# Output projection and first gate of a two-layer decoder trunk: plain products in place of block products

## The chip, the cores and the metric

One core of one Trainium2 chip runs the whole program in one launch. Times are device microseconds (us), the median over runs. TensorE is PE, VectorE is DVE, ScalarE is ACT, GpSimd is POOL, and SP issues most of the DMAs.

## The reference

Two layers over 1024 positions of width 1024, float32 throughout. `u` is a root-mean-square norm of `h`:

```
proj  = u @ w_in[i]                        # 8 forgetting-attention heads, 8 retention heads
mixed = concat(fox_attention(...), silu(rg) * group_norm(retention(...)))
h = h + mixed @ w_out[i]                   # output projection, 1024 x 1024
up = rms_norm(h, ffn_norm_w[i]) @ w_up[i]  # 1024 x 5632, halves a and g
h = h + (gelu(causal_conv3(a)) * g) @ w_down[i]
gate = sigmoid(rms_norm(h, ple_norm_w[i]) @ w_ple_gate[i])   # 1024 x 1024
h = h + gate * (p[i] @ w_ple_proj[i])
```

After the second layer there is a last norm of `h`.

## The kernel before

Everything lies feature-major: `h` is eight slices of 128 features x 1024 positions. A float32 product is made of three products of rounded parts, high by high, low by high and high by low, so every operand is split into two (`xh`, `xl`; `wh`, `wl`; `uh`, `ul`; `dh`, `dl`): the high part by a cast on ACT, the low part by a subtraction, on DVE or POOL as the table behind `E(name, i)` says (one letter per index: V is DVE, G is POOL).

There are two kinds of product. A **plain product** (`dense_fm`) makes one output slice of 128 features out of 8 input slices: 8 x 6 matmuls of 512 columns into a PSUM tile `d` of 128x1024; its weights come ready in order from `weights()`, which loads and splits them four ahead. A **block product** (`g_parts`, `parts`) makes two output slices (a "quarter" q of four) with seven half-size products in place of eight. The seven, `NAMES`, each take for every pair of input slices three matmuls of 512 columns. The weight side is made by a `Line` of steps (`Fixed`): raw weights `wr`, sums `ws` on POOL, then high part `wh` on ACT and low part `wl` on DVE. The moving side of a pair of slices is a `Joined`: four builds with subtractions (`t`) and splits (`x`, `xh`, `xl`) on ACT and DVE. `join` adds the seven half results, 128x512 each, out of PSUM into `h` on DVE; `form` puts them together in a new tile.

A layer runs: input projections (plain) woven with attention and retention by `weave`, where the tuple `DENSE` is the order of the dense pieces and `SPANS` says between which positions in it each of the four attention and four retention pairs is spread; the output projection; the MLP's up product (block); its down product in four groups of input pairs (block); the gate; and the norm's sums of squares (`Stats`, tiles `hsq` and `ssq`) along the way. The second layer's gate is plain, with moving sides by `make_u` (`uh`, `ul` of a slice); the first layer's is a block product. The output projection is done in two halves of its input: the attention heads' half, `g_out`, is the last piece "wo0" of `DENSE` and so woven with the last retention pair; the retention heads' half follows after it. `h` goes to DRAM (`hs_dram`) and is read back for the down product, and once more for the first gate. The tile framework's scheduler decides the order on each engine out of the order in which the program is written and the room that tiles need.

Nearly all instructions are issued by one helper at line 145, so groups in the profile are told apart by their tiles.

Of the kernel before, what the change touches and what calls it, by code (L numbers as in the profile page):

```python
# [9 lines left out]
F32 = mybir.dt.float32  # L10
# [7 lines left out]
DEPTH = 2  # L18
# [16 lines left out]

DENSE = ("fi1", "rv0", "fi2", "fv1", "fi3", "ri0", "rv1", "rg0", "ri1", "ri2", "rg1", "ri3", "ep0", "em0", "wo0")
SPANS = ((6, 42.6), (42.6, 79.9), (85.9, 123.5), (130.4, 145.5), (138.9, 199.2), (194.7, 197.7), (217.3, 254.5), (251.1, 300.0))

# [121 lines left out]
def trunk(ctx, tc, ap):  # L160
# [48 lines left out]
    def weight_order():  # L209
        V, G_ = nc.vector, nc.gpsimd  # L210
        for l in range(DEPTH):
            qk = lambda j: (ap["wqk"][l, j], KC, P, E("qk", j))
            tm = lambda j: [(ap["wtm"][l, j, i], 4, 256, E("tm", 2 * j + i)) for i in range(2)]
            fv0 = [(ap["wfv"][l][:, a:b, :], b - a, FVW, G_) for a, b in FVK]
            specs = {"ep": lambda i: [], "wo": lambda i: [],
                     "fi": lambda i: [qk(i), qk(4 + i)], "fv": lambda i: tm(0), "ri": lambda i: [qk(8 + i), qk(12 + i)],
                     "rv": lambda i: tm(1 + i), "rg": lambda i: tm(3 + i),
                     "em": lambda i: [(ap["wproj"][l, j], 8, P, E("em", j)) for j in range(2)]}
# [693 lines left out]
    for l in range(DEPTH):  # L912
# [119 lines left out]

        def hand(now, then):

            def after(n):
                for m in now:
                    m.drop(n)
                for m in then:
                    m.build(n)
            return after  # L1040

        def specs():
            for half in range(2):
                for q in range(4):
                    yield ap["wout"][l, half, q], 2
# [6 lines left out]
            if l + 1 < DEPTH:  # L1052
                for q in range(4):
                    yield ap["wgate"][l, q], 4

        def g_out():

            nonlocal line, u, rb
            u = rb = None
            del pr[:], ret_tab[:]  # L1060
            line = Line(specs())
            for p in range(2):
                mx.append(Joined(mixed[2 * p], mixed[2 * p + 1]))
                mixed[2 * p:2 * p + 2] = [None, None]
            for q in range(4):
                for m in (2 * q, 2 * q + 1):
                    h[m] = G("h")
                    nc.sync.dma_start(h[m], h_dram[m])
                to = h[2 * q:2 * q + 2]
                yield from g_parts(line, mx, lambda name, s: join(name, s, to))  # L1070

        fox_ops, ret_ops, ret_v, ret_tab, vst, tail = {}, {}, {}, [], [], []
        pr, mx, h, line = [], [], [None] * KC, None
        pp = dr.tile([KC, P, T], F32, name="pp")
        raw = []
        for name in ("qs", "ks"):
# [3 lines left out]
            if name == "qs":  # L1080
# [8 lines left out]
                  "ep": lambda i: g_load_embed(),  # L1089
                  "em": lambda i: g_embed(), "wo": lambda i: g_out()}  # L1090
        units = [(a, e, 27.0, lambda i=i: fox(i)) for i, (a, e) in enumerate(SPANS[:4])]
# [4 lines left out]
        ret_v.clear()  # L1096
        del vst[:]


        def scales(which, p):  # L1100
            return nw[:, which, 2 * p:2 * p + 1], nw[:, which, 2 * p + 1:2 * p + 2], minus[:, which, 2 * p + 1:2 * p + 2]

        stats = Stats()
        mx = [Joined(mixed[2 * p], mixed[2 * p + 1]) for p in (2, 3)]
        mixed = None
        u = []
        hs_dram = dr.tile([KC, P, T], F32, name="hs")
        for q in range(4):
            to = h[2 * q:2 * q + 2]
            parts(line, mx, lambda name, s: join(name, s, to), hand(mx, []) if q == 3 else None)  # L1110
            u.append(Joined(*to, scales(2 * NW_FFN + l, q)))
            for m in (2 * q, 2 * q + 1):
# [3 lines left out]
        to = None  # L1116

# [50 lines left out]
        for g, mx in enumerate(stored):  # L1168
            then = stored[g + 1] if g + 1 < len(stored) else []
            for q in range(4):  # L1170
                if g == 0:
                    for m in (2 * q, 2 * q + 1):
                        h[m] = G("h")
                        nc.sync.dma_start(h[m], hs_dram[m])
                to = h[2 * q:2 * q + 2]
                if q == 3:
                    for m in then:
                        m.load(0)

                def after(n):  # L1180
                    for m in mx:
                        m.drop(n)
                    for m in then:
                        m.build(n)
                        if n < 3:
                            m.load(n + 1)
                    if not then and not ends:
                        u[2].build(n)
# [10 lines left out]
                if not then and not ends:  # L1199

                    for m in range(2 * q - 2 if q == 3 else 2 * q, 2 * q + 2):
                        if q != 2:
                            h[m] = None
        mx = then = stored = to = None


        if not ends:
            nstats = Stats()
            h_dram = dr.tile([KC, P, T], F32, name="hd")
            rb = None  # L1210
            old, u = u, []
            for q in range(4):
                sg = [G("sg") for i in range(2)]
                for m in (2 * q, 2 * q + 1):
                    h[m] = G("h")
                    nc.sync.dma_start(h[m], hs_dram[m])

                def scale_s(i):
                    nonlocal rb, stats
                    if rb is None:  # L1220
                        _, rb = stats.finish()
                        stats = None
                    return rb

                def after(n):
                    for m in old:
                        m.drop(n)
                    if n:
                        u.extend(make_u(h[m], nw[:, 2 * NW_ATTN + l + 1, m:m + 1]) for m in (2 * n - 2, 2 * n - 1))
                    if n == 2:  # L1230
                        fetch()
                parts(line, old, lambda name, s: form(name, s, sg, scale_s), after if q == 3 else None)
                for i in range(2):
                    m = 2 * q + i
                    pt = G("ppt")
                    nc.sync.dma_start(pt, pp[m])
                    nc.scalar.activation(sg[i], sg[i], AF.Sigmoid)
                    nc.gpsimd.tensor_tensor(sg[i], sg[i], pt, op=ALU.mult)
                    nc.vector.tensor_tensor(h[m], h[m], sg[i], op=ALU.add)
                    if q == 3:  # L1240
                        u.append(make_u(h[m], nw[:, 2 * NW_ATTN + l + 1, m:m + 1]))
                    nstats.add(h[m], sg[i])
                    nc.sync.dma_start(h_dram[m], h[m])
                    if q == 3:
                        h[m] = None
                sg = pt = None
            stats, nstats = nstats, None
            h = rb = old = None

    fetch()  # L1250

# [126 lines left out]
```

## Time and profile before

| | |
|---|---|
| median of 3 runs | 2899.47 us (2892.65 to 2899.89) |
| the profiled execution | 2898.59 us, of which the span is 2896.8 us |
| mean granted TensorE clock | 0.97 of full speed |
| PE busy | 2717.5 us, 94%, 13718 matmuls |
| DVE busy | 2086.6 us, 72% |
| ACT, POOL busy | 1226.5 us (42%), 902.0 us (31%) |

The shares are means over stages that differ. The stages lie about so in the span: layer 0's attention and retention up to 580 us, the second half of its output projection 580 to 690, its MLP to 1290, its gate to 1460; layer 1's to 2028, 2028 to 2137, to 2737, and its gate and the last norm behind that.

### The profile page before, as it was taken

The page shows a single profiled execution, that of the slowest core. Times are in us where ns is not written, and L with a number is a line of the kernel's source. Part 1 is how long each engine was busy: PE and PEld are TensorE (multiplying, and loading weights), DVE is VectorE, ACT ScalarE, POOL GpSimd, SP SyncE. Part 2 cuts the span into 40 slices and gives each one's busy share as a digit, 9 for nine tenths or more (in the row PEclk, how much of TensorE's full clock was granted, in tenths as well). Part 3 has the DMA queues.
Part 4 walks back from the last instruction along what each step waited for, and adds up shares of the span by engine and source line. Part 5 has one row for each costly group of instructions (what it writes and reads, how often), then busy time and mean ns, then how long its engine had stood idle before and what let it go on. Part 6 is the DMA issues. An engine that isn't in the chain of part 4 may idle for free. (4 is left out here: it accounts for less than half of the span.)

```text
span 2896.8 us, 36327 instructions
## 1 busy us (share of the span) xinstructions
PE 2717.5 (94%) x13718; PEld 2263.5 (78%) x13718; DVE 2086.6 (72%) x3031; ACT 1226.5 (42%) x1824; POOL 902.0 (31%) x652
## 2 busy tenths in 40 slices
PE   8988999978999998997889989999799999989998
PEld 7887989757888887775678879897578888867776
DVE  4565645898887778779745556458978877787786
ACT  4354543444344333435434545424443433434352
POOL 3222332223233323434432222322232333234240
PEclk9999999999999999998989999999999999999999
DMA  5333122422323236433533331224223232364242
GB/s 161 88 81 95 54 61 71 158 76 95 109 99 113 95 132 213 153 95 120 178 91 88 81 97 52 62 72 154 77 95 109 99 112 96 137 208 151 87 146 98
DMA packets 116864, 315.77 MB, mean 109 GB/s; under 512 B 13520, under 2 KB 34512, under 8 KB 116688
## 3 DMA queue, kind: packets, MB, share of 16 engines
q1 hardware_dynamic: 113616, 305.05, 32.4%
q10 hardware_dynamic: 3072, 8.39, 1.2%
q8 instruction: 108, 1.77, 0.3%
q14 instruction: 68, 0.56, 0.1%
HBM read 210.04 MB, written 69.80 MB: 97 GB/s over the span
## 5 line engine op out<-in xcount | busy, mean ns | idle before, releaser
L145 POOL TENSOR_TENSOR ws<-wr 128x512 f32<-128x512 f32 (+2 forms) x192 | 285.7, 1495 | 1049.6 <-PE d L145 520.6
L145 PE MATMUL s<-xh,wh 128*128 128x512 f32 x936 | 377.8, 406 | 25.6 <-ACT wh L145 13.2
L145 PE MATMUL d<-xh,wh 128*128 128x512 f32 x936 | 374.8, 404 | 20.2 <-DVE h L145 12.6
L145 PE MATMUL s<-xl,wh 128*128 128x512 f32 x936 | 377.4, 403 | 11.2 <-DVE xl L145 11.2
L145 PE MATMUL s<-xh,wl 128*128 128x512 f32 x936 | 372.0, 403 | 6.1 <-DVE wl L145 5.7
L145 PE MATMUL d<-xl,wh 128*128 128x512 f32 x936 | 373.6, 399 | 2.4 <-DVE xl L145 2.4
L145 PE MATMUL d<-xh,wl 128*128 128x512 f32 x936 | 370.6, 399 | 0.0
L145 POOL TENSOR_TENSOR ws<-ws,wr 128x512 f32<-128x512 f32 (+2 forms) x192 | 262.9, 1370 | 104.2 <-issue 55.6
L145 PE MATMUL d<-x,w 128*128 128x512 f32 x936 | 246.2, 399 | 22.4 <-ACT x L145 8.8
L145 ACT CAST wh<-ws 128x1024 fp32r<-128x1024 f32 (+2 forms) x192 | 168.5, 888 | 219.8 <-POOL ws L145 203.6
L145 DVE TENSOR_TENSOR wl<-ws,wh 128x1024 fp32r<-128x1024 f32 (+2 forms) x192 | 218.3, 1146 | 40.7 <-ACT wh L145 31.9
L145 PE MATMUL d<-dh,uh 128*128 128x256 f32 (+1 forms) x768 | 222.1, 290 | 22.8 <-DVE vst L145 11.2
L145 PEld LDWEIGHTS s<-xh,wh 128*128 128x128 f32 x936 | 180.0, 192 | 76.3 <-ACT wh L145 20.5
L145 PEld LDWEIGHTS d<-xh,wh 128*128 128x128 f32 x936 | 178.9, 191 | 71.5 <-DVE h L145 21.0
L145 PEld LDWEIGHTS d<-x,w 128*128 128x128 f32 x936 | 175.3, 190 | 71.1 <-ACT x L145 10.1
L145 PEld LDWEIGHTS s<-xl,wh 128*128 128x128 f32 x936 | 180.5, 193 | 54.8 <-DVE xl L145 14.3
L145 PEld LDWEIGHTS s<-xh,wl 128*128 128x128 f32 x936 | 180.0, 192 | 54.5 <-DVE wl L145 13.3
L145 PE MATMUL d<-dl,uh 128*128 128x256 f32 (+1 forms) x768 | 221.8, 289 | 0.0
L145 PE MATMUL d<-dh,ul 128*128 128x256 f32 (+1 forms) x768 | 220.8, 288 | 0.0
L145 PE MATMUL d<-uh,dh 128*128 128x512 f32 (+1 forms) x584 | 197.6, 407 | 18.1 <-ACT dh L145 11.1
L145 PEld LDWEIGHTS d<-xl,wh 128*128 128x128 f32 x936 | 179.6, 192 | 43.7 <-DVE xl L145 3.0
L145 PEld LDWEIGHTS d<-xh,wl 128*128 128x128 f32 x936 | 178.9, 191 | 42.2
(209 smaller groups left out, 5863.3 us busy)
## 6 DMA issues: line engine op xcount, KB each, us to landing
wr<-in_wup_dram SPq DMA_DIRECT2D x88, 512.0 KB, 3.8
zz<-zd SPq DMA_DIRECT2D x66, 512.0 KB, 3.7
wr<-in_wdown_dram SPq DMA_DIRECT2D x48, 384.0 KB, 4.2
zd<-z SPq DMA_DIRECT2D x66, 256.0 KB, 2.0
dr<-in_wqk_dram SPq DMA_DIRECT2D x32, 512.0 KB, 3.5
hs<-h SPq DMA_DIRECT2D x24, 512.0 KB, 2.6
h<-hs SPq DMA_DIRECT2D x24, 512.0 KB, 4.8
zd<-t SPq DMA_DIRECT2D x22, 512.0 KB, 3.9
```

The source lines that it names most:

```text
L145: ins = f(*[bare(v) for v in a], **{n: bare(v) for n, v in k.items()})
```

## The change

The output projection of both layers and the gate of the first become plain products. "wo0" leaves `DENSE` and the last retention pair's span in `SPANS` shrinks with it. All eight `mixed` slices are split into `mxh`, `mxl` (four low parts on POOL, by an entry that the table has, `mx="GVVGVGGV"`), and eight plain products follow; after each odd slice the block sides (`Joined`) for the MLP are built for the two finished slices, and the MLP's weight `Line` begins at slice 4. Behind the down product both layers now make the gate's sides with `make_u`, keep `h` in place, and call `fetch()` at the third quarter. In the gate, the result of the first two slices is copied out of PSUM by ACT, and the product with `ppt` is on DVE. The weights are laid out to match.

```
-DENSE = (..., "ri3", "ep0", "em0", "wo0")
-SPANS = (..., (217.3, 254.5), (251.1, 300.0))
+DENSE = (..., "ri3", "ep0", "em0")
+SPANS = (..., (217.3, 254.5), (251.1, 259.3))
...
+            yield from [(ap["wout"][l, m], KC, P, E("wo", m)) for m in range(KC)]
             yield None
-            for i in range(len(PIECES) if l + 1 == DEPTH else 0):
-                yield from [(ap["wlast"][0, m], KC, P, E("gate%d" % l, i * KC + m)) for m in range(KC)]
+            for i in range(len(PIECES) if l + 1 == DEPTH else 1):
+                yield from [(ap["wgate"][l, m], KC, P, E("gate%d" % l, i * KC + m)) for m in range(KC)]
...
+        mx = []
+        for c in range(8):
+            mx.append((G("mxh", F32R), G("mxl", F32R)))
+            split(*mx[c], mixed[c], E("mx", c))
+            mixed[c] = None
+        mixed = None
         stats = Stats()
-        mx = [Joined(mixed[2 * p], mixed[2 * p + 1]) for p in (2, 3)]
...
-        for q in range(4):
-            to = h[2 * q:2 * q + 2]
-            parts(line, mx, lambda name, s: join(name, s, to), hand(mx, []) if q == 3 else None)
-            u.append(Joined(*to, scales(2 * NW_FFN + l, q)))
-            for m in (2 * q, 2 * q + 1):
-                stats.add(h[m], G("hsq"))
-                nc.sync.dma_start(hs_dram[m], h[m])
-                h[m] = None
+        for m in range(KC):
+            h[m] = G("h")
+            nc.sync.dma_start(h[m], h_dram[m])
+            if m == 4:
+                line = Line(specs())
+            elif m > 4:
+                line.step()
+            d = dense_fm(weights(), mx)
+            if m == KC - 1:
+                mx = None
+            nc.vector.tensor_tensor(h[m], d, h[m], op=ALU.add)
+            nc.sync.dma_start(hs_dram[m], h[m])
+            stats.add(h[m], G("hsq"))
+            if m % 2:
+                s1 = slice(m - 1, m)
+                s2 = slice(m, m + 1)
+                u.append(Joined(h[m - 1], h[m], (nw[:, 2 * NW_FFN + l, s1], nw[:, 2 * NW_FFN + l, s2], minus[:, 2 * NW_FFN + l, s2])))
+                h[m - 1:m + 1] = [None, None]
...
                 if not then:
-                    if ends:
-                        u += [make_u(h[m], nw[:, 2 * NW_PLE + l, m:m + 1]) for m in (2 * q, 2 * q + 1)]
-                    else:
-                        u.append(Joined(*to, scales(2 * NW_PLE + l, q), q != 2))
+                    u += [make_u(h[m], nw[:, 2 * NW_PLE + l, m:m + 1]) for m in (2 * q, 2 * q + 1)]
                     for m in (2 * q, 2 * q + 1):
                         stats.add(h[m], G("hsq"), None, E("hsq", m))
-                        if not ends:
-                            nc.sync.dma_start(hs_dram[m], h[m])
...
+                    if q == 2:
+                        fetch()
...
-                parts(line, old, lambda name, s: form(name, s, sg, scale_s), after if q == 3 else None)
-                for i in range(2):
-                    m = 2 * q + i
-                    pt = G("ppt")
-                    nc.sync.dma_start(pt, pp[m])
-                    nc.scalar.activation(sg[i], sg[i], AF.Sigmoid)
-                    nc.gpsimd.tensor_tensor(sg[i], sg[i], pt, op=ALU.mult)
-                    nc.vector.tensor_tensor(h[m], h[m], sg[i], op=ALU.add)
...
+            for m in range(KC):
+                pt = G("ppt")
+                nc.sync.dma_start(pt, pp[m])
+                d = dense_fm(weights(), u)
+                if m == 0:
+                    _, rb = stats.finish()
+                    stats = None
+                sg = G("sg")
+                if m < 2:
+                    nc.scalar.copy(sg, d)
+                nc.vector.tensor_tensor(sg, sg if m < 2 else d, rb, op=ALU.mult)
+                nc.scalar.activation(sg, sg, AF.Sigmoid)
+                nc.vector.tensor_tensor(sg, sg, pt, op=ALU.mult)
+                nc.vector.tensor_tensor(h[m], h[m], sg, op=ALU.add)
+                then.append(make_u(h[m], nw[:, 2 * NW_ATTN + l + 1, m:m + 1]))
+                nstats.add(h[m], sg)
+                nc.sync.dma_start(h_dram[m], h[m])
+                h[m] = None
```

What it moves on the engines, at three places. The first is PE in layer 0, in the last retention pair (`qn`, `kz`, `rv`, `state`, `sm` are its chunks). Before:

```order
L145 MATMUL d<-xh,wh 128x512
L145 MATMUL d<-xl,wh 128x512
L145 MATMUL d<-xh,wl 128x512
L145 MATMUL s<-qn,kz_5178 128x128
L145 MATMUL s<-qn,kz_5179 128x128
L145 MATMUL s<-rv,kt 128x128
L145 MATMUL s<-state,qn 128x128
L145 MATMUL s<-rv,sm 128x64 x2
L145 MATMUL d<-xh,wh 128x512
L145 MATMUL d<-xl,wh 128x512
L145 MATMUL d<-xh,wl 128x512
L145 MATMUL d<-xh,wh 128x512
```

and with the change, some of the same chunks:

```order
L145 MATMUL s<-qn,kz_5179 128x128
L145 MATMUL s<-state,qn 128x128
L145 MATMUL s<-rv,kt 128x128
L145 MATMUL s<-rv,sm 128x64 x2
L145 MATMUL s<-state,qn 128x128
L145 MATMUL s<-rv,sm 128x64 x2
L145 MATMUL s<-qn,kz_5178 128x128
L145 MATMUL s<-qn,kz_5179 128x128
L145 MATMUL s<-rv,kt 128x128
L145 MATMUL s<-state,qn 128x128
L145 MATMUL s<-rv,sm 128x64 x2
L145 MATMUL s<-qn,kz_5178 128x128
```

The 512-column products of the output projection (`xh`, `wh`) that stood between the chunks are gone, and chunk follows chunk.

The second is DVE in layer 0 in the second half of the output projection (the number behind a tile's name is its buffer). Before, half results (128x512) going into several slices of `h` with the block side of the first slices between them:

```order
L145 TENSOR_TENSOR h_5533<-h_5533,d_6003 128x512
L145 TENSOR_TENSOR h_5396<-h_5396,s_5903 128x512
L145 TENSOR_TENSOR h_5394<-h_5394,d_5892 128x512
L145 SCALAR_TENSOR_TENSOR x_5965<-h_5394,nw_84,x_5965 128x512
L145 TENSOR_TENSOR h_5535<-h_5535,s_6014 128x512
L145 TENSOR_TENSOR h_5533<-h_5533,d_6003 128x512
L145 TENSOR_TENSOR h_5394<-h_5394,s_5903 128x512
L145 TENSOR_TENSOR h_5396<-h_5396,d_5892 128x512
L145 SCALAR_TENSOR_TENSOR t2_5970<-h_5394,nw_84,t34_5971 128x512
```

and with the change, one plain result (128x1024) for a slice, the low part of a weight, and then the block side of the pair:

```order
L145 TENSOR_TENSOR h_5689<-d_5697,h_5689 128x1024
L145 TENSOR_TENSOR dl_5851<-dr_5848,dh_5850 128x1024
L145 SCALAR_TENSOR_TENSOR t2_5756<-h_5689,minus_66,t2_5756 128x512
L145 SCALAR_TENSOR_TENSOR t34_5757<-h_5689,nw_84,t34_5757 128x512
L145 TENSOR_TENSOR ssq_5537<-ssq_5537,hsq_5748 128x1024
L145 SCALAR_TENSOR_TENSOR xl_5764<-h_5689,nw_84,xh_5763 128x512
L145 SCALAR_TENSOR_TENSOR t34_5757<-h_5689,minus_66,t2_5756 128x512
L145 SCALAR_TENSOR_TENSOR xl_5771<-h_5689,nw_84,xh_5770 128x512
L145 TENSOR_TENSOR xl_5755<-t2_5756,xh_5754 128x1024
L145 TENSOR_TENSOR xl_5764<-t34_5757,xh_5763 128x512
```

One sum of 128x1024 has taken the place of the half sums, and a whole side follows in one piece.

The third is PE at the end of the first gate with the change, where the next layer's first products begin (`uh_11465` and `ul_11466` are made from the gate's last slice; rows of the same product for other slices stand ahead of these):

```order
L145 MATMUL d_11480<-uh_11396,dh_11407 128x512 x2
L145 MATMUL d_11480<-ul_11397,dh_11407 128x512 x2
L145 MATMUL d_11480<-uh_11396,dl_11408 128x512 x2
L145 MATMUL d_11562<-uh_10981,dh_11476 128x512 x2
L145 MATMUL d_11562<-ul_10982,dh_11476 128x512 x2
L145 MATMUL d_11562<-uh_10981,dl_11477 128x512 x2
L145 MATMUL d_11480<-uh_11465,dh_11407 128x512 x2
L145 MATMUL d_11562<-uh_11051,dh_11476 128x512 x2
```

The next layer's second product `d_11562` begins before the first, `d_11480`, has its last input. In the change's order 48 matmuls of 512 columns stand between the gate's last matmul and the first use of `uh_11465`.

## Rows read from the trace of the kernel before

**Rows 1.** The page's first line and its busy times with shares of the span and instruction counts.

```profile
span 2896.8 us, 36327 instructions
...
PE 2717.5 (94%) x13718; PEld 2263.5 (78%) x13718; DVE 2086.6 (72%) x3031; ACT 1226.5 (42%) x1824; POOL 902.0 (31%) x652
```

**Rows 2.** Busy time of each engine by stretch: from:to in us, length, then PE (with the count of matmuls), PEld, DVE, ACT and POOL busy us with counts, mean granted TensorE clock, DMA share and GB/s.

```profile
700.00:1000.00 300.00, 300.00 (x1297) 242.92 (x1296) 236.93 (x233) 116.01 (x140) 94.17 (x60) 1.00 0.30 107
...
580.00:690.00 110.00, 87.87 (x339) 64.60 (x338) 101.01 (x140) 53.69 (x78) 36.47 (x28) 0.91 0.24 82
1290.00:1365.00 75.00, 60.93 (x221) 43.93 (x219) 69.31 (x92) 38.93 (x55) 25.44 (x18) 0.89 0.32 109
1365.00:1460.00 95.00, 78.67 (x326) 62.32 (x326) 71.75 (x60) 44.51 (x51) 47.53 (x23) 0.90 0.45 158
...
2028.00:2137.00 109.00, 86.84 (x333) 63.83 (x333) 100.84 (x139) 53.24 (x78) 36.16 (x28) 0.91 0.23 82
2200.00:2500.00 300.00, 300.00 (x1297) 243.19 (x1296) 238.57 (x232) 115.14 (x138) 101.28 (x64) 1.00 0.30 106
2737.00:2812.00 75.00, 69.97 (x307) 53.97 (x306) 63.11 (x68) 38.27 (x45) 30.75 (x19) 1.00 0.39 136
```

**Rows 3.** PE by line and tile from 580 to 690 us, the small matmuls alone: out<-in, shapes, count, busy us and mean ns, idle before.

```profile
L145 PE MATMUL s<-ones,ssq 128*128 128x1 f32 x16 | 1.8, 245 | 0.0
L145 PE MATMUL s<-ident,rc 128*128 128x128 f32 x11 | 1.4, 275 | 0.0
L145 PE MATMUL s<-ident,yn 128*128 128x128 f32 x8 | 1.2, 275 | 1.8 <-DVE yn L145 1.8
```

**Rows 4.** The same view from 1290 to 1460 us, the small matmuls alone.

```profile
L145 PE MATMUL s<-ident,rc 128*128 128x128 f32 x16 | 1.9, 275 | 0.0
L145 PE MATMUL s<-ones,ssq 128*128 128x1 f32 x16 | 1.9, 251 | 0.0
```

**Rows 5.** DVE by line and tile from 580 to 690 us, the same columns.

```profile
L145 DVE TENSOR_TENSOR xl<-t,xh 128x512 fp32r<-128x512 f32 (+1 forms) x17 | 16.8, 1002 | 0.0
L145 DVE TENSOR_TENSOR h<-h,d 128x512 f32<-128x512 f32 x22 | 14.7, 676 | 0.7 <-PE d L145 0.7
...
L145 DVE TENSOR_TENSOR ssq<-ssq,hsq 128x1024 f32<-128x1024 f32 x7 | 8.5, 1212 | 0.0
L145 DVE SCALAR_TENSOR_TENSOR t<-h,nw,t 128x512 f32<-128x512 f32 x8 | 7.4, 931 | 0.0
L145 DVE SCALAR_TENSOR_TENSOR xl<-h,nw,xh 128x512 fp32r<-128x512 f32 x8 | 6.4, 803 | 0.0
L145 DVE SCALAR_TENSOR_TENSOR t<-h,minus,t 128x512 f32<-128x512 f32 x8 | 5.9, 741 | 0.0
...
L145 DVE SCALAR_TENSOR_TENSOR x<-h,nw,x 128x512 fp32r<-128x512 f32 x4 | 3.4, 859 | 0.0
```

**Rows 6.** Waits of PE from 580 to 690 us: who waited on whom, us, times, and the longest.

```profile
PE d L145 <- ACT x L145: 4.1, 1, 4.1
PE s L145 <- DVE h L145: 3.3, 2, 2.5
PE s L145 <- ACT wh L145: 2.9, 1, 2.9
```

**Rows 7.** The same from 1290 to 1460 us.

```profile
PE d L145 <- DVE ul L145: 5.7, 1, 5.7
PE d L145 <- DVE sg L145: 5.4, 1, 5.4
```

**Rows 8.** Groups of the whole run by line, engine, operation and tile: count, busy us and mean ns, idle before and its releasers.

```profile
L145 DVE TENSOR_TENSOR wl<-ws,wh 128x1024 fp32r<-128x1024 f32 (+2 forms) x192 | 218.3, 1146 | 40.7 <-ACT wh L145 31.9 <-PE s L145 8.6
...
L145 POOL TENSOR_TENSOR dl<-dr,dh 128x1024 fp32r<-128x1024 f32 (+2 forms) x51 | 127.6, 2506 | 243.7 <-ACT dh L145 209.8 <-issue 12.8 <-DMA sw<-raw 7.4
L145 DVE TENSOR_TENSOR wl<-wr,wh 128x1024 fp32r<-128x1024 f32 (+2 forms) x96 | 113.5, 1182 | 24.7 <-ACT wh L145 22.1 <-PE d L145 2.3
...
L145 DVE TENSOR_TENSOR w<-wr,w 128x512 fp32r<-128x512 f32 (+2 forms) x96 | 82.3, 859 | 26.8 <-ACT w L145 26.4
...
L145 DVE TENSOR_TENSOR dl<-dr,dh 128x1024 fp32r<-128x1024 f32 x27 | 42.2, 1565 | 33.8 <-ACT dh L145 21.1 <-issue 12.7
...
L145 DVE TENSOR_TENSOR h<-h,sg 128x512 f32<-128x512 f32 (+2 forms) x25 | 30.2, 1209 | 9.1 <-POOL sg L145 8.5
...
L145 DVE SCALAR_TENSOR_TENSOR sm<-triangle,s 128x256 f32<-128x256 f32 x64 | 26.3, 411 | 9.3 <-PE s L145 9.2
...
L145 DVE SCALAR_TENSOR_TENSOR ul<-h,nw,uh 128x1024 fp32r<-128x1024 f32 x16 | 23.8, 1490 | 4.4 <-ACT uh L145 4.3
...
L145 DVE TENSOR_TENSOR state<-state,gain 128x128 f32<-128x128 f32 x48 | 22.2, 463 | 0.1
...
L145 ACT ACTIVATE uh<-h,nw 128x1024 fp32r<-128x1024 f32 x16 | 18.3, 1148 | 26.1 <-DVE h L145 25.0 <-PE d L145 1.0
...
L145 DVE TENSOR_TENSOR state<-s,state 128x128 f32<-128x128 f32 x48 | 13.8, 288 | 39.2 <-PE s L145 38.1
...
L145 DVE TENSOR_TENSOR sg<-sg,rb 128x512 f32<-128x512 f32 (+1 forms) x8 | 9.7, 1220 | 0.7 <-ACT rb L145 0.7
```

**Rows 9.** POOL's timeline around 507 us: start, duration, operation, and in brackets the wait before it.

```profile
507.62 2.78 POOL L145 TENSOR_TENSOR qn<-qn,dec 128x1024 f32<-128x1024 f32 x1 [2.23 <-DVE qn L145]
```

**Rows 10.** The view of the tile `mixed`: count, shortest, median and longest ns, first and last start.

```profile
L145 DVE TENSOR_TENSOR xl<-mixed,xh x16: 674/684/2891, 508.1 to 2054.4; 128x512 fp32r<-128x512 f32 x16
```

More of the change, by code (lines that the diff above doesn't have):

```diff
@@ L1031, in ret @@
             return g_retention(*ret_ops.pop(pair), v, lambda: ret_v["rg"][pair], mixed[4 + pair], tail)
[L1033 to L1040, printed above, removed]
         def specs():
-            for half in range(2):
-                for q in range(4):
-                    yield ap["wout"][l, half, q], 2
             for j in range(FC // 2):
@@ L1051, in specs @@
                     yield ap["wdown"][l, q][:, :, :, group[0] * P:(group[-1] + 1) * P], len(group)
[L1052 to L1065, printed above, removed]
-                for m in (2 * q, 2 * q + 1):
-                    h[m] = G("h")
-                    nc.sync.dma_start(h[m], h_dram[m])
-                to = h[2 * q:2 * q + 2]
-                yield from g_parts(line, mx, lambda name, s: join(name, s, to))
         fox_ops, ret_ops, ret_v, ret_tab, vst, tail = {}, {}, {}, [], [], []
-        pr, mx, h, line = [], [], [None] * KC, None
+        pr, h = [], [None] * KC
         pp = dr.tile([KC, P, T], F32, name="pp")
@@ L1089, in trunk @@
                   "ep": lambda i: g_load_embed(),
-                  "em": lambda i: g_embed(), "wo": lambda i: g_out()}
+                  "em": lambda i: g_embed()}
         units = [(a, e, 27.0, lambda i=i: fox(i)) for i, (a, e) in enumerate(SPANS[:4])]
@@ L1096, in trunk @@
         ret_v.clear()
-        del vst[:]
-        def scales(which, p):
-            return nw[:, which, 2 * p:2 * p + 1], nw[:, which, 2 * p + 1:2 * p + 2], minus[:, which, 2 * p + 1:2 * p + 2]
+        del vst[:], pr[:], ret_tab[:]
+        u = rb = None
+        mx = []
[4 more added lines that the diff above has]
+        mixed = None
         stats = Stats()
-        mx = [Joined(mixed[2 * p], mixed[2 * p + 1]) for p in (2, 3)]
-        mixed = None
+        hs_dram = dr.tile([KC, P, T], F32, name="hs")
         u = []
-        hs_dram = dr.tile([KC, P, T], F32, name="hs")
-        for q in range(4):
-            to = h[2 * q:2 * q + 2]
-            parts(line, mx, lambda name, s: join(name, s, to), hand(mx, []) if q == 3 else None)
-            u.append(Joined(*to, scales(2 * NW_FFN + l, q)))
-            for m in (2 * q, 2 * q + 1):
-                stats.add(h[m], G("hsq"))
-                nc.sync.dma_start(hs_dram[m], h[m])
-                h[m] = None
-        to = None
+        for m in range(KC):
[16 more added lines that the diff above has]
+                h[m - 1:m + 1] = [None, None]
         zd = [dr.tile([4, P, T], F32, name="zd%d" % j, bufs=1) for j in range(FC // 2)]
@@ L1209, in trunk @@
             h_dram = dr.tile([KC, P, T], F32, name="hd")
[L1210 to L1231, printed above, removed]
-                parts(line, old, lambda name, s: form(name, s, sg, scale_s), after if q == 3 else None)
-                for i in range(2):
-                    m = 2 * q + i
-                    pt = G("ppt")
-                    nc.sync.dma_start(pt, pp[m])
-                    nc.scalar.activation(sg[i], sg[i], AF.Sigmoid)
-                    nc.gpsimd.tensor_tensor(sg[i], sg[i], pt, op=ALU.mult)
-                    nc.vector.tensor_tensor(h[m], h[m], sg[i], op=ALU.add)
[L1240 to L1246, printed above, removed]
@@ L1247, in trunk @@
-            stats, nstats = nstats, None
-            h = rb = old = None
-    fetch()
+            then = []
+            for m in range(KC):
[16 more added lines that the diff above has]
+                h[m] = None
@@ L1253, in final_norm @@
+            u, then, stats, nstats = then, None, nstats, None
+            h = rb = pt = sg = None
     def final_norm(pstats, at, c):
@@ L1357 @@
         wtm=np.stack([_units(w) for w in (fv[:, :, 256:], rv[:, :, :256], rv[:, :, 256:], rg[:, :, :256], rg[:, :, 256:])], 1),
-        wout=_quads(a["w_out"].reshape(DEPTH * 2, D // 2, D)).reshape(DEPTH, 2, 4, 2, P, 2, 2 * P),
+        wout=_cols(a["w_out"]),
         wup=_quads(a["w_up"]),
-        wgate=_quads(a["w_ple_gate"][:1]),
-        wlast=_cols(a["w_ple_gate"][1:]),
+        wgate=_cols(a["w_ple_gate"]),
         wdown=_quads(a["w_down"]),
```

12 lines of the change are left out of this document (3 added, 9 removed).

## The prediction

> **What bounds the kernel now.** I read the page's busy shares first, then the same shares stretch by stretch, then the PE lines and waits of the stretches in which PE is not full, and last the DVE lines there. PE is busy 94% of 2896.8 us [rows 1]. The whole run says only that PE is the engine to look at; the stretches say where a change can pay [rows 2]. In the middle of the MLP (700–1000 and 2200–2500) PE runs 300.00 of 300 us at a granted clock of 1.00, and 1297 matmuls pass: 300 / 1297 = 0.2313 us per 512-column matmul. This is the price of a matmul wherever PE is full. In four other stretches PE has holes and the clock sinks to 0.89–0.91, and there I call lost whatever the stretch takes beyond its matmuls at 0.2313 us (small ones at half of that, 0.1157; this takes in the lower clock):
> - second half of the output projection, layer 0 (580–690): 339 matmuls, of which 16 + 11 + 8 = 35 are small [rows 3]; 110 − 304 × 0.2313 − 35 × 0.1157 = 35.6 us lost. Layer 1 (2028–2137): 333, 109 − 298 × 0.2313 − 4.0 = 36.1 us.
> - first gate (1290–1460): 221 + 326 matmuls, 32 small [rows 4]; 170 − 515 × 0.2313 − 3.7 = 47.2 us.
>
> So 119 us are lost at just the three products that the change rewrites.
>
> Why they are lost: in 580–690 DVE is busy 101.01 of 110 us [rows 2], so DVE is the bound there. Per quarter q of the second half PE has 42 matmuls, 9.7 us. DVE has seven half-product sums into h at 0.676 (4.7), the block side of two h slices (7.4 + 5.9 + 6.4 + 3.4, and some 12 of the 17 `xl<-t` at 1.0, all over four pairs: 8.8), two `ssq` sums (2.4) [rows 5], and one weight step: low parts and copies of the block weights take 218.3 + 113.5 + 82.3 = 414 us in the run [rows 8] over 2 × (8 + 22 + 16) + 4 = 96 steps, 4.3 us (an upper value, the output projection's steps are half as deep). That is up to 20 us of DVE against 9.7 of PE. PE's waits name the same: `h` on DVE, `x` and `wh` on ACT [rows 6]. In the gate PE waits 5.7 us on `ul` and 5.4 on `sg` once each [rows 7]: the passage into the next layer, where nothing covers the chain from the last `sg` to the first `u`.
>
> **The change, part by part.**
> *More matmuls.* A block product of 4 quarters × 7 halves × 12 = 336 becomes 8 × 8 × 6 = 384: +48, three times, +144 × 0.2313 = **+33.3 us**. Nothing can hide this where PE is full.
>
> *Output projection.* DVE per pair of slices afterwards: h sums out of PSUM 4 × 0.676 = 2.7, weight low parts 2 × 1.565 = 3.1 [rows 8], side 8.8, `ssq` 2.4 = 17.0 us, against 96 matmuls = 22.2 us of PE. PE becomes the longer one. The block side of `mixed` goes too. From slice 4 on the MLP's first weight steps are added (4 × 4.3 = 17): slices 4–7 then have 34 + 17 = 51 us of DVE against 44.4 of PE, a backlog of some 7 us, part of which lands behind the last slice. What of the 36 us stays lost:
> - The last retention pair. Half of the output projection was woven through it; now some six of its eight chunks stand with no dense product between them. DVE needs 0.463 + 0.288 + 0.411 = 1.16 us per chunk [rows 8], PE about 0.7 for six small matmuls. Bounds: 0, if other queued work covers it; 10, if each of eight chunks adds 1.2 us. I take 4: the DVE rate less the PE rate over eight chunks (8 × 0.46).
> - The first plain product needs all eight `mixed`; the last pair's come latest, but 42 of its 48 matmuls (9.7 us) go ahead. Four low parts are on POOL at 2.5 us each [rows 8]. Bounds 0 and 5 (two in a row), I take 1.
> - The tail: the last pair's side and the backlog, covered by some 33 matmuls (7.6 us) of the first MLP step on earlier pairs. Bounds 0 and 10 (8.8 + 7 + one sum and hand-overs, less 7.6), I take 5, the middle, as the backlog is shared with POOL and ACT.
>
> Together 10 (0 to 25) stay, so each layer gets back 36 − 10 = **−26 us**, less than the 36 but more than the 11.1 it pays.
>
> A `mxl` on POOL can also stop a DVE instruction: the first `xl<-mixed,xh` beside POOL's 2.78 us `qn` took up to 2.89 us where the median is 0.684 [rows 9, 10]. At about 2.2 us for each of four this is at most 9 us of DVE, with PE still fed by queued matmuls; I take nothing of it, and it lies inside the bounds above. The Trainium skill, "SBUF — State Buffer", section "Who interferes with whom", says that a DVE instruction with two SBUF inputs and a GpSimd instruction that reads SBUF exclude each other for a whole instruction; by that rule all four would be blocked, and these rows agree for one of them.
>
> *First gate.* The last layer's gate is already plain and has `make_u` sides. Its passage 2737–2812 shows what such a gate leaves lost: 307 matmuls, 32 taken as small as in the first gate: 75 − 275 × 0.2313 − 3.7 = 7.7 us [rows 2]. The end of the gate is new: the chain from the last slice to the next layer's `u` is scaling 1.22, sigmoid about 1.1 (as `uh`), product about 1.2, sum 1.21, `uh` 1.15, `ul` 1.49 [rows 8] = 7.4 us; the order puts 48 matmuls (11.1 us) ahead of the first use of the last `u`. So that is hidden with 3.7 us to spare. Left: 7.7 + about 1 = 9 (5 to 20, the upper end if the old waits of 5.7 and 5.4 stay). 47 − 9 = **−38 us**. The store and reload of h for the gate go away; they were seen by no PE wait and count nothing. Multiplying by `ppt` moves from POOL (off DVE's path) to DVE, 8 × 1.2 = 10 us over 89 us of PE: hidden by the freed sums.
>
> *Fetching one quarter earlier in the last layer*: 0 to −2, I take 0. *Middle of the MLP*: the same rows with one or two matmuls shifted; PE was full and DVE 237 of 300 [rows 2], so 0.
>
> Sum: 2898.6 + 33.3 − 2 × 26 − 38 = 2841.9. The profiled run (2898.59) is 0.9 under the median (2899.47), so **2843 us**. Best bounds: 2898.6 + 33.3 − 72 − 42 = 2818. Worst: 2898.6 + 33.3 − 2 × 11 − 27 = 2883.
>
> **The rivals.**
> - *The covers are too thin.* The upper bounds come true: retention stands bare, the DVE backlog lands behind slice 7. For it: DVE's 51 against 44 us in slices 4–7, and that every dense row has gone from the last retention run. Against it: layer by layer some 9.7 and 7.6 us of matmuls stand ahead of the two turns. About **2883**.
> - *A wait repeated in the MLP's steps* (the other side). The scheduler's order of the 22 block steps per layer shifts by a row or two; if a weight or a sum comes late in each of the 44, all gain goes when each costs (2898.6 − 2841.9) / 44 = 1.3 us. Where the old output projection waited on a weight or an operand, one wait took 2.9 (`wh`) and 4.1 us (`x`) [rows 6]; at 4.1 us in half of the steps it is 2841.9 + 22 × 4.1 = **2932**. Against it: 700–1000 and 2200–2500 without any hole, DVE at 79%.
> - *PE is the bound everywhere.* If the lost time at these places is only the price of changing stages, as the DVE and ACT work of the next stage is still in front, the added matmuls are paid and the holes move on: 2898.6 + 33.3 = **2932**. Against it: DVE 101 of 110 and falling to 17 per 22. By the Trainium skill, "Perfetto Trace Analysis", section "Identifying the Most-Contended Engine", the engine with the highest occupancy is the one to relieve first; TensorE at 94% (weight loads 78%) would be it, and this change loads it more, so the rule taken over the whole run speaks for 2932. The trace of these stretches does not bear it out, since there DVE is the fuller one.
> - *Neither*: half of the saving goes, about 2898 (the losses that stay are 30 + 30 + 26).
>
> **How the numbers follow.** The chance of the forecast (2818 to 2868) is 0.66, of thin covers (2868 to 2890) 0.13, of no difference 0.05, of the MLP wait 0.10, of the PE price 0.06. About 0.3% (8.7 us) is what a measurement of this kernel can tell from no change. So faster 0.79, same 0.05, slower 0.16. The first two cases hold 0.79; the range is their bounds, 2815 (2818 less the earlier fetch) to 2888.
>
> **What the profile after would show.** Right, if 580–690's counterpart has DVE well under 0.9 and a clock near 1.0, if the waits on `ACT x` and `ACT wh` are gone there, and if the gate has no 5 us wait at its end. The bare retention shows as PE's waits on `sm` or `state` before the first `d<-mxh`, the tail as a wait on the last pair's `xl`. Wrong would be any regular hole in 700–1000 or 2200–2500, or PE waiting on `mxl` for more than 5 us.

## The result and the profile after

The changed kernel takes 2849.58 us (median of 4 runs, 2847.20 to 2851.58) against 2897.24 us of the kernel before (4 runs, 2892.65 to 2899.89): a ratio of 0.983, 95% interval 0.982 to 0.984, 47.7 us less. The forecast was 2843 us, 56.7 us less than the median known when it was made (2899.47), with a range of 2815 to 2888.

The page of the changed kernel's profiled execution, its span and busy times:

```profile
span 2849.8 us, 35986 instructions
...
PE 2717.4 (95%) x13862; PEld 2279.5 (80%) x13862; DVE 1930.3 (68%) x2760; ACT 1171.7 (41%) x1706; POOL 811.2 (28%) x579
```

Against [rows 1] there are 144 more matmuls, and PE is busy as long as before (2717.4 against 2717.5 us): what the added matmuls take is given back by a higher clock, whose mean went from 0.970 to 0.981. DVE is busy 156 us less. Busy time by stretch, with the columns of [rows 2]:

```profile
510.00:556.00 46.00, 38.97 (x221) 32.55 (x220) 30.76 (x54) 21.72 (x26) 10.19 (x5) 0.96 0.47 157
556.00:650.00 94.00, 93.08 (x406) 75.16 (x405) 58.93 (x60) 37.62 (x48) 17.74 (x9) 1.00 0.34 122
650.00:680.00 30.00, 28.21 (x131) 22.77 (x131) 18.12 (x21) 11.53 (x18) 7.61 (x5) 0.94 0.17 56
700.00:1000.00 300.00, 300.00 (x1297) 243.18 (x1296) 239.23 (x232) 114.91 (x138) 100.18 (x64) 1.00 0.30 107
1290.00:1320.00 30.00, 26.02 (x94) 18.84 (x93) 27.54 (x36) 14.42 (x19) 12.27 (x9) 0.89 0.14 44
1320.00:1440.00 120.00, 119.13 (x543) 97.74 (x542) 68.58 (x57) 49.77 (x50) 27.16 (x12) 1.00 0.38 128
...
1966.00:2056.00 90.00, 89.60 (x390) 72.45 (x389) 53.58 (x57) 32.63 (x41) 14.19 (x9) 1.00 0.29 106
2056.00:2086.00 30.00, 27.98 (x131) 22.65 (x130) 20.28 (x22) 13.10 (x18) 8.69 (x6) 0.94 0.15 53
2745.00:2760.00 15.00, 9.94 (x52) 8.45 (x51) 5.62 (x6) 5.15 (x6) 2.38 (x2) 0.77 0.66 245
```

The output projections (556–650 and 1966–2056) now run with PE full and a granted clock of 1.00, DVE at 58.93 of 94 us; in their old place DVE had 101.01 of 110 and the clock 0.91 [rows 2]. The MLP's middle still passes 1297 matmuls in 300 us. Of these stretches the clock is below full in layer 0's embedding (510–556: 0.96), in the turn into the MLP (650–680, 2056–2086: 0.94), at the beginning of the first gate (0.89) and, new, for 15 us at the last layer's gate (2745–2760: 0.77; in the same place before it was 1.00 [rows 2]).

The time by stage, from one landmark to the next in each profiled execution. The landmarks are the starts of the first instruction of a kind in a layer: the embedding's first matmul (`d<-ph,dh`), the MLP's first `z<-d,conv`, the down product's first `h<-h,d`, the gate's first `h<-h,sg`.

| stage, us | before | after | difference |
|---|---|---|---|
| layer 0 up to the embedding | 513.3 | 512.0 | -1.2 |
| embedding, output projection, first MLP step | 206.2 | 193.4 | **-12.8** |
| MLP up product | 390.0 | 388.1 | -1.8 |
| down product to the gate's first sum | 275.0 | 265.7 | **-9.3** |
| rest of the gate, layer 1 up to the embedding | 576.6 | 559.9 | **-16.7** |
| embedding, output projection, first MLP step | 205.9 | 189.3 | **-16.6** |
| MLP up product | 389.8 | 388.1 | -1.7 |
| down product to the last gate's first sum | 255.5 | 265.2 | **+9.8** |
| last gate and norm, to the end | 84.6 | 87.9 | **+3.3** |

These make up the difference of the spans, 47.0 us. The four stages that hold the three rewritten products give back 55.4 us; the last gate, of which only the fetch was moved, takes 13 us (10 us in the trace of the changed kernel's second measurement, `after_again` below).

### The profile page after: what moved, and what is told of

It reads as the page before. It is cut to its first block, busy times and chain, and to the rows that moved or that the text cites. A ratio compares the mean times of both kernels' runs of the same rounds, so it can differ in the third digit from the quotient of the medians.

```text
span 2849.8 us, 35986 instructions
## 1 busy us (share of the span) xinstructions
PE 2717.4 (95%) x13862; PEld 2279.5 (80%) x13862; DVE 1930.3 (68%) x2760; ACT 1171.7 (41%) x1706; POOL 811.2 (28%) x579
## 5 line engine op out<-in xcount | busy, mean ns | idle before, releaser
L145 POOL TENSOR_TENSOR ws<-wr 128x512 f32<-128x512 f32 (+2 forms) x152 | 229.9, 1519 | 909.2 <-PE d L145 576.2
L145 PE MATMUL s<-xh,wh 128*128 128x512 f32 x792 | 315.7, 399 | 15.4 <-ACT xh L145 10.0
L145 PE MATMUL s<-xl,wh 128*128 128x512 f32 x792 | 314.8, 397 | 9.4 <-DVE xl L145 9.3
L145 PE MATMUL s<-xh,wl 128*128 128x512 f32 x792 | 310.0, 398 | 4.2 <-DVE wl L145 4.2
L145 PE MATMUL d<-xl,wh 128*128 128x512 f32 x792 | 313.1, 395 | 0.0
L145 PE MATMUL d<-xh,wh 128*128 128x512 f32 x792 | 310.3, 396 | 2.3 <-DVE h L145 2.2
L145 PE MATMUL d<-xh,wl 128*128 128x512 f32 x792 | 310.0, 396 | 0.0
L145 PE MATMUL d<-uh,dh 128*128 128x512 f32 (+1 forms) x712 | 235.9, 403 | 16.6 <-ACT dh L145 8.7
L145 POOL TENSOR_TENSOR dl<-dr,dh 128x1024 fp32r<-128x1024 f32 (+2 forms) x58 | 142.3, 2456 | 327.9 <-ACT dh L145 268.1
L145 PE MATMUL d<-ul,dh 128*128 128x512 f32 (+1 forms) x712 | 233.9, 397 | 0.6 <-DVE ul L145 0.6
L145 PE MATMUL d<-uh,dl 128*128 128x512 f32 (+1 forms) x712 | 229.8, 394 | 0.8 <-POOL dl L145 0.7
## 6 DMA issues: line engine op xcount, KB each, us to landing
wr<-in_wup_dram SPq DMA_DIRECT2D x88, 512.0 KB, 3.9
zz<-zd SPq DMA_DIRECT2D x66, 512.0 KB, 3.7
dr<-in_wqk_dram SPq DMA_DIRECT2D x32, 512.0 KB, 3.5
dr<-in_wgate_dram SPq DMA_DIRECT2D x24, 512.0 KB, 3.7
zd<-t SPq DMA_DIRECT2D x22, 512.0 KB, 2.7
```

The lines of the kernel that those rows point to most:

```text
L145: ins = f(*[bare(v) for v in a], **{n: bare(v) for n, v in k.items()})
```

## The experiments

Every run is compared with runs of the kernel before on its own chip (medians 2897.7 to 2900.0 us over the three sets of runs).

**Each part alone.** The kernel before with the plain output projection:

```
-DENSE = (..., "em0", "wo0")
+DENSE = (..., "em0")
-        for q in range(4):
-            parts(line, mx, ...)
+        for m in range(KC):
+            d = dense_fm(weights(), mx)
...
```

> The kernel before with the plain output projection of the changed kernel in both layers; the first gate stays a block product, and the last layer's fetch stays where it was. Theory (DVE bounds the old output projection and PE the new one): the losses beyond the matmul price fall by some 26 us in layer 0 and 29 us in layer 1, as the changed kernel's profile shows, and 48 matmuls are paid in each layer, 11.1 us: -15 and -17, so about 2865 us against 2897. Rival (the block product's losses are the price of changing stages, and matmuls are always paid): +22, about 2919. If the two parts help each other through the shared order of work, the sum of this run's gain and of gate_only's gain differs from the whole gain of 47.7 us by more than 5 us.

Measured: 2859.21 us (2858.08 to 2869.67), ratio 0.9865 (0.9843 to 0.9887), some 40 us less. And with the plain gate alone, with its sides and the earlier fetch:

```
-                parts(line, old, lambda name, s: form(name, s, sg, scale_s), after if q == 3 else None)
+                d = dense_fm(weights(), u)
+                    if q == 2:
+                        fetch()
...
```

> The kernel before with the plain first gate (and the sides made by make_u, and the earlier fetch in both layers) of the changed kernel; the output projections stay block products. Theory: -36 us of losses at the gate, +11.1 us for 48 matmuls, and some +9 us at the last layer's gate from the earlier fetch: about -16, so 2881 us. Rival (the plain output projection is what set the gate's gain free, or the gate's holes only move): 2897 + 11 = 2908 us.

Measured: 2880.61 us, ratio 0.9929 (0.9910 to 0.9947), as the theory had it. Both parts pay by themselves, which is against the rival that the matmuls are paid and the holes move on. Their gains add up to 60 us, though, 10 to 12 more than the two together (50.5 and 47.7 in the two measurements). The spans of the traced executions do add up: 28.9 and 17.1 us less than before, 46.0 together, against 47.0 for the whole change. But the traced execution of the first took 2869.67 us, 10 to 12 us more than its other three, so no trace shows where their excess lies; this stays open.

**Which engine bounds the output projection.** Four runs add either PE work or DVE work to the same product, in the old form and in the new. DVE work on the kernel before, and on the changed one:

```
+            for m in (2 * q, 2 * q + 1):
+                nc.vector.tensor_tensor(h[m], h[m], h[m], op=ALU.max)
```

> The kernel before with eight more DVE instructions of 128x1024 (a maximum of h with itself, which changes nothing) in the second half of each layer's output projection, about 8 x 1.2 = 9.7 us of DVE a layer and no other work. Theory (DVE bounds that stretch): nearly all of it shows, +15 to +20 us over the two layers, about 2914 us. Rival (PE and the change of stages bound it): 0 to +4 us.

> The changed kernel with the same eight DVE instructions in each layer's output projection, one behind each slice's sum. Theory (PE bounds the plain product, DVE has about 5 us to spare per pair in the first half and only the end is tight): 0 to +8 us over the two layers, about 2853 us, less than half of what they cost the kernel before. Rival (DVE still bounds the stretch): +15 to +20 us, about 2867.

PE work on the kernel before (`again=4` in the second half of the output projection) and on the changed one:

```
-            for p, x in enumerate(moving):
+            turns = [0] * (part < again) + list(range(len(moving)))
+            for turn, p in enumerate(turns):
```

```
-            d = dense_fm(weights(), mx)
+            d = dense_fm_twice(weights(), mx)
...
+        for n, k in enumerate((0, 0, 1, 2, 3, 4, 5, 6, 7)):
```

> The kernel before with 48 more matmuls of 512 columns in the second half of each layer's output projection (the first pair's three matmuls once more in four of the seven half products of each quarter, which adds that pair's part twice to the result), and no other work. Theory (DVE bounds that stretch): PE has 35 us to spare there, 0 to +6 us over both layers in place of 2 x 11.1 = 22.2. Rival (each matmul is paid): +22 us, about 2919.

> The changed kernel with 48 more matmuls of 512 columns in each layer's output projection (the first of the eight input slices once more in each product, which adds that slice's part twice to the result), and no other work. Theory (PE bounds the plain product): +2 x 11.1 = +22 us less some us of waits at the end that the longer product covers, +16 to +22, about 2869 us. Rival (DVE still bounds it): 0 to +6 us.

| added in the two output projections | time, us | against the same kernel without it | stage with the output projection, layer 0 and 1 |
|---|---|---|---|
| before, 16 DVE instructions (19.4 us) | 2927.40 | **+28** | 221.6 and 215.6 (206.2, 205.9 without) |
| after, the same 16 | 2852.54 | **+3** | 195.1 and 192.7 (193.4, 189.3) |
| before, 96 matmuls (22.2 us) | 2897.08 (ten runs, 2885.99 to 2899.46) | **-2** | 206.1 and 205.3 |
| after, 96 matmuls | 2871.59 | **+22** | 203.3 and 199.4 |

(Against the second measurement of the changed kernel, 2847.20 us, its two figures are 2.4 larger.) The four form a cross: the old form pays for DVE and not for PE, the new one for PE and little for DVE. One thing they leave untested: the added DVE instruction also stands between a slice's sum and its block side, so in the old form a longer chain and a full engine would look alike; that DVE is busy 101.01 of 110 us there speaks for the full engine. The kernel before with 48 more matmuls in each layer's second half, by stretch:

```profile
582.00:692.00 110.00, 95.48 (x385) 71.41 (x385) 104.39 (x140) 54.08 (x78) 37.98 (x28) 0.95 0.24 82
2030.00:2139.00 109.00, 96.40 (x385) 72.26 (x384) 103.46 (x140) 53.82 (x78) 38.23 (x28) 0.94 0.24 82
```

Stretches of the same length as in [rows 2] hold 385 matmuls in place of 339 and 333, with DVE still at 104.39 and 103.46 us; the stages of the table have not grown. The kernel before with more DVE work:

```profile
580.00:705.00 125.00, 91.07 (x331) 65.07 (x330) 109.53 (x146) 53.39 (x79) 40.08 (x28) 0.84 0.20 70
2040.00:2160.00 120.00, 88.94 (x328) 63.87 (x327) 116.18 (x149) 54.28 (x80) 34.01 (x28) 0.86 0.20 69
```

and PE's longest waits there in layer 0, where the first of them had been 4.7 us before (580–690):

```profile
PE d L145 <- DVE h L145: 4.7, 5, 2.3
```

```profile
PE d L145 <- DVE h L145: 10.6, 5, 4.5
PE s L145 <- ACT wh L145: 7.8, 3, 4.4
PE d L145 <- DVE x L145: 3.5, 1, 3.5
```

The wait on `h` is 10.6 us in place of 4.7, and the clock is 0.84 and 0.86 in place of 0.91. For 9.7 us of DVE the stage of layer 0 is 15.4 us longer and that of layer 1 9.7 us: what DVE is late costs its own length in one layer and more in the other. Why they differ isn't shown.

**The last gate.** Where a part of the 13 us goes is seen in the timelines of the changed kernel (start, duration, operation, and in brackets the wait before it). PE at the place where the norm's sum `ssq` has been added up and its scale `rc` is wanted:

```profile
2746.86 1.95 PE L145 MATMUL s<-ones,ssq 128*128 128x1 f32 x16 [0.41 <-DVE ssq L145]
...
2749.69 0.39 PE L145 MATMUL d<-uh,dl 128*128 128x512 f32 x1
2754.73 3.78 PE L145 MATMUL s<-ident,rc 128*128 128x128 f32 x16 [4.66 <-POOL rc L145]
```

DVE there:

```profile
2751.65 1.23 DVE L145 TENSOR_TENSOR dl<-dr,dh 128x1024 fp32r<-128x1024 f32 x1 [4.84 <-ACT dh L145]
2752.79 0.16 DVE L145 TENSOR_SCALAR rc<-s 128x8 f32<-128x8 f32 x1
2754.20 1.22 DVE L145 TENSOR_TENSOR dl<-dr,dh 128x1024 fp32r<-128x1024 f32 x1 [1.25 <-ACT dh L145]
```

and ACT, which casts the gate's weights:

```profile
2750.57 1.04 ACT L145 CAST dh<-dr 128x1024 fp32r<-128x1024 f32 x1 [7.50 <-DMA dr<-in_wgate_dram]
2753.07 1.04 ACT L145 CAST dh<-dr 128x1024 fp32r<-128x1024 f32 x1 [1.45 <-DMA dr<-in_wgate_dram]
```

ACT waits 7.50 us for a weight's DMA, DVE 4.84 us for ACT, with the low part `dl` of that weight at the head of its queue. The 0.16 us `rc` stands behind it, though the sum that it reads was there at 2746.86 + 1.95 = 2748.81, 4 us before `rc` began. Then come POOL and PE, which stands for 4.66 us and then runs its 16 small matmuls at a lower clock. Test: the fetch of the last layer where it had been.

```
-                    if q == 2:
+                    if q == 2 and not ends:
                         fetch()
...
+    fetch()
```

> The changed kernel with one edit: in the last layer the fetch of the gate's weights comes behind the whole down product again, in place of behind its third quarter; layer 0 keeps the earlier one. Theory (the changed kernel's PE waits 4.7 us on rc at the last gate since DVE holds a weight's low part, whose DMA is late, ahead of the small sum for rc, and runs at a lower clock behind it): about -9 us, 2841 us against 2850, with PE's wait on rc near 1 us as in the kernel before. Rival (the loss there comes from the other order of the down product and not from the fetch): within 2 us of the changed kernel.

Measured: 2835.33 us, ratio 0.9777 (0.9759 to 0.9795). The changed kernel, unaltered, in the last set of runs took 2847.20 us, ratio 0.9829:

> The changed kernel, unaltered, on the chip of the three runs sent with it, for a direct comparison with them. If chips differ by little: 2850 us, within 0.3%.

so the edit is worth some 12 us. In its trace the last two stages take 258.1 and 84.9 us, 10 us less than in the changed kernel's (7 us less than in its second trace). DVE at the same place, with its fetch late:

```profile
2736.84 3.09 DVE L145 TENSOR_TENSOR dl<-dr,dh 128x1024 fp32r<-128x1024 f32 x1 [0.27 <-issue]
2739.85 0.15 DVE L145 TENSOR_SCALAR rc<-s 128x8 f32<-128x8 f32 x1
2744.80 1.23 DVE L145 TENSOR_TENSOR dl<-dr,dh 128x1024 fp32r<-128x1024 f32 x1 [4.80 <-ACT dh L145]
```

and PE's 16 small matmuls on `rc`:

```profile
2741.78 2.05 PE L145 MATMUL s<-ident,rc 128*128 128x128 f32 x16 [0.93 <-POOL rc L145]
```

DVE waits as long for ACT as in the changed kernel (4.80 us), but `rc` now stands ahead of that `dl` and not behind it, and PE waits 0.93 us in place of 4.66. What the edit changed is the place in DVE's queue, not the wait.

The earlier fetch costs at a second place too, 38 us ahead of this one, in the last step of the down product. PE, DVE and POOL in the changed kernel:

```profile
2716.39 1.21 PE L145 MATMUL d<-x,w 128*128 128x512 f32 x4 [2.24 <-DVE w L145]
```

```profile
2713.77 2.56 DVE L145 TENSOR_TENSOR w<-wr,w 128x256 fp32r<-128x256 f32 x1
```

```profile
2712.68 3.37 POOL L145 TENSOR_TENSOR dl<-dr,dh 128x1024 fp32r<-128x1024 f32 x1
```

The first low part of the gate's weights now runs on POOL beside DVE's `w`, which takes 2.56 us, and PE waits 2.24 us on it; the clock is 0.74 from 2715 to 2720 us and 0.91 from 2720 to 2725. With the late fetch the same `w` takes 0.96 us, PE waits 0.38 us ahead of the same product, and the clock is 1.00 from 2700 to 2720:

```profile
2705.24 0.96 DVE L145 TENSOR_TENSOR w<-wr,w 128x256 fp32r<-128x256 f32 x1
```

All fourteen traces of this document fall in two groups by these two waits. In the six with the earlier fetch PE waits 4.5 to 5.7 us on `rc` and 2.2 to 2.3 us ahead of this product, in the eight with the late one 0.5 to 0.9 and 0.4 to 1.5. What of the 13 us lies outside the two places isn't itemized.

**The embedding.** PE's waits in the changed kernel from 510 to 680 us:

```profile
PE d L145 <- ACT ph L145: 3.6, 1, 3.6
PE s L145 <- DVE xl L145: 1.8, 1, 1.8
PE s L145 <- DVE sm L145: 1.2, 1, 1.2
PE d L145 <- DVE pl L145: 1.0, 1, 1.0
...
PE d L145 <- POOL mxl L145: 0.4, 1, 0.4
```

The longest is none that the forecast named: `ph`, the embedding's input.

```
-DENSE = (..., "rg1", "ri3", "ep0", "em0")
+DENSE = (..., "rg1", "ep0", "ri3", "em0")
```

> The changed kernel with one edit: in DENSE the loading of the embedding's input, ep0, stands one piece earlier, ahead of ri3. Theory (in layer 0 PE waits 3.6 us on ph, whose DMA comes late, with nothing of the output projection left to run meanwhile, and the clock is at its lower level behind it for some 4 us): the wait goes, -5 to -8 us, about 2843 us. Rival (the wait is for the SP queue as a whole, or the rooms taken earlier hold other work up): 0 to +5 us.

Measured: 2826.39 us, ratio 0.9742 (0.9725 to 0.9759), 21 us below the unaltered kernel's second measurement, against the 5 to 8 of the theory. PE's waits from 500 to 680 us:

```profile
PE d L145 <- ACT ppt L145: 3.2, 2, 2.5
PE s L145 <- DVE xl L145: 1.9, 1, 1.9
PE s L145 <- DVE sm L145: 0.8, 1, 0.8
```

The wait on `ph` is gone, and those on `ppt`, two in both, come to 3.2 us where the changed kernel had 1.0. The stages say that the gain isn't there alone: against the unaltered kernel traced in the last set, 2.6 and 0.9 us in layer 0 up to and through the output projection, 6.2 about its down product (where the unaltered kernel's own two traces are 2.4 apart), 3.9 in layer 1 ahead of the embedding, 2.4 about its down product. Is it the change that makes room for it?

> The kernel before with ep0 one piece earlier in DENSE, and nothing else. Theory (there the first half of the output projection was woven in behind the embedding and gave PE work while ph was late): 0 to -5 us, so the changed kernel's wait on ph is of the change's making. Rival (the embedding's input is late in both kernels alike, and the edit is worth the same without the change): -20 us or more.

Measured: 2886.73 us, ratio 0.9959 (0.9943 to 0.9975), 11 us less: neither the 0 to 5 of the theory nor the 20 of the rival. The kernel before had waited too, though the output projection was woven in behind:

```profile
PE d L145 <- ACT ph L145: 2.8, 1, 2.8
```

So about half of the gain is had without the change. In its stages 9.3 us are gained in layer 0 through the output projection and 16.9 in layer 1 before and through it, while both MLP up products are 4 us longer and layer 0's down product 4.9. One place in `DENSE` moves the order of much that follows; which of it gives the gain, here or in the changed kernel, is not settled.

**Both edits.**

> The changed kernel with both edits: the last layer's fetch behind the whole down product, and ep0 one piece earlier in DENSE. Theory (two separate losses, one at the last gate, one at the embedding in either layer): the gains add up, -14 to -16 us for the fetch and -24 us for ep0 as measured singly, about 2812 us. Rival (both are partly one thing, such as room that comes free earlier, or the difference between two chips): no better than the better of the two, about 2825 us.

Measured: 2815.73 us (2810.42 to 2817.96), ratio 0.9717 (0.9699 to 0.9735), 31.5 us below the changed kernel and 82 below the kernel before: near the sum of the two (12 + 21), and not the 2825 of the rival. This is the fastest form found. With slice 7's sum of squares on POOL beside:

```
-            stats.add(h[m], G("hsq"))
+            stats.add(h[m], G("hsq"), None, nc.gpsimd if m == 7 else None)
```

> As late_early, and the last slice's sum of squares in the output projection goes to POOL (2.4 us there) in place of DVE (1.2 us). Theory (what is left at the turn into the MLP is DVE's chain behind slice 7, where PE waits some 2 us on xl and the clock is at its lower level for 3 to 4 us more): -1 to -3 us a layer, 2 to 6 in all against late_early. Rival (POOL's sums of MLP weights come later by as much, and rc with them): 0 to +5 us.

Measured: 2819.95 us, ratio 0.9736 (0.9719 to 0.9753). The intervals overlap; the 2 to 6 us hoped for are not there, the 4 us more lie in the rival's 0 to 5, and taking 1.2 us off DVE at the turn into the MLP is no gain.

## Why the prediction was right, and where it was not

- *The price of a matmul*, 0.2313 us, held: +22 us for 96 matmuls in the changed kernel, +24 against its second measurement (22.2 by the price).
- *DVE bounds the old output projection, PE the new one*: shown in both directions by the four added loads; whether the old form is held by a full DVE or by the chain that runs through it is argued and not tested.
- *Output projection, -26 + 11.1 = -15 a layer*: the stage moved by -12.8 and -16.6, and by -12.9 and -13.6 with the output projection alone changed.
- *What stays of its losses* was 10 us by the forecast, and the sum came out about right with a wrong list, which is luck. The bare retention was priced at 4 us and shows one wait of 1.2 us on `sm`; the first plain product waits 0.4 us on `mxl` (1 taken); the tail is a wait of 1.8 us on `xl` with the clock at 0.94 for 30 us (5 taken: 30 − 99 × 0.2313 − 32 × 0.1157 = 3.4 us lost there, as 32 of the 131 matmuls are small). The embedding's 3.6 us on `ph` and 1.0 on `pl` were not in it: they stood in the trace of before ahead of 580 us, at 2.8 and 0.6, and the stretches were chosen behind them. In layer 0 these waits and the 3.4 us come to at most 9.6 us of the 11.7 that its stage kept (35.6 − 11.1 − 12.8); the clock of 0.96 from 510 to 556 can account for about 2 more.
- *First gate, -38 + 11.1 = -27*: -9.3 and -16.7 in its two stages, -26, and -11.9 and -17.1 with the gate alone changed. Neither the wait on `ul` nor that on `sg` [rows 7] is left; PE's largest from 1260 to 1440 us are these:

```profile
PE d L145 <- DVE w L145: 2.3, 1, 2.3
PE s L145 <- ACT wh L145: 1.5, 3, 0.9
```

- *Middle of the MLP, 0*: -1.8 and -1.7 us for the up products, and 700–1000 without a hole. The waits of the second rival did not come.
- *Fetching earlier in the last layer, 0 to -2*: this is the step that failed. It cost 10 to 13 us in the two last stages, and moving it back gave some 12 back. The forecast gave no reason for its 0. It did not ask what the fetched weights' low parts meet: on DVE one stands in front of `rc`, whose input was ready, and on POOL one runs beside DVE's `w`. With 12 us for it the forecast would have been 2855, 5 us off on the other side: what it put at nothing or left out (layer 0 up to the embedding and the up products, -4.7 us together) goes the other way.
- *The rivals*: the third (PE is the bound everywhere, matmuls are only paid) falls by each part alone and by the added matmuls before, which cost nothing. The first (covers too thin) would have shown in the two output projections, and they gave back what was forecast.

## What to carry to other kernels

A busy share over the whole run hid that the engine which bounds differs by stage; counting, stage by stage, what the time exceeds the busiest engine's nominal work showed where more matmuls cost nothing. A cheaper form in matmuls can be the dearer one if its sums and sides go to an engine that is full already, and adding a known load to either engine tells which it is. A transfer that starts earlier also puts its first consumer earlier into an engine's queue: look at what stands behind it there, and at what runs beside it on another engine.

## What the runs showed of the hardware

16 DVE instructions of 1.21 us, 19.4 us, made the kernel before 28 us longer, of which 25.1 us lie in the two stages with the output projection (15.4 and 9.7), with the granted clock falling from 0.91 to 0.84 and 0.86 in the two stretches; and 96 more matmuls in the same stretches cost nothing there, with the clock at 0.95 and 0.94. At the last gate the 16 small matmuls behind PE's wait of 4.66 us took 3.78 us, and in the kernel with the late fetch, behind a wait of 0.93 us, 2.05 us.

DVE was also held by POOL there, as [rows 9, 10] had shown once: in the changed kernel a sum of squares of 1.21 us took 3.42 us beside a `dl` of 2.58 us that POOL had begun 0.24 us earlier:

```profile
2743.39 3.42 DVE L145 TENSOR_TENSOR ssq<-ssq,hsq 128x1024 f32<-128x1024 f32 x1
```

```profile
2743.15 2.58 POOL L145 TENSOR_TENSOR dl<-dr,dh 128x1024 fp32r<-128x1024 f32 x1 [4.84 <-ACT dh L145]
```

Both read two operands from SBUF. The Trainium skill, "SBUF — State Buffer", section "Who interferes with whom", has this as an exclusive lock: whichever starts first holds the other off for the whole instruction. The trace agrees: 2743.15 + 2.58 = 2745.73, and DVE's instruction ends at 2746.81, 1.08 us later, close to its own length. DVE's `w` of 2.56 us at the last down product ends at 2716.33, 0.28 us behind POOL's `dl`. The other side is in the trace as well: 52 sums `h<-h,d` and `h<-h,s`, which read one operand from PSUM, began with at least 0.6 us of a POOL instruction still to run, and took less than 0.01 us longer on average than their shortest.

Of the four low parts of `mixed` on POOL, of which the forecast feared up to 9 us of DVE, three held a DVE instruction up in each layer, by some 1.1, 2.2 and 2.2 us. PE waited 0.4 us on POOL's `mxl`, and none of the three is among its waits there.
